# A two-layer decoder trunk on one core: the second block's weights into empty slots, three state sums side by side, and weight sums behind a subtraction

## The chip, the core and the metric

The kernel runs on one core of a Trainium2 chip. The metric is the device time of one execution in microseconds (us), as a median over runs. A core has a matrix engine (TensorE, PE in the rows; its weight loads are PEld), a vector engine (VectorE, DVE), a scalar engine (ScalarE, ACT), GpSimd (POOL) and a queue that issues transfers (SyncE, SP). Each engine works through its own instructions in a fixed order, and an instruction that waits holds up everything behind it on that engine. Matrix products land in PSUM, which has eight banks of 128 x 512 fp32.

## The reference

Two layers run over 592 tokens: 16 learned meta tokens, 8 sample sequences of 8 tokens, and a prompt of 512. The width is 1024 and everything is fp32. Layer 0 has an mLSTM and a retention mixer of four heads each, layer 1 an HGRN2 mixer; behind each mixer stands a ConvFFN of 2816 channels.

```python
xn = rms_norm(x, norm_mix[0])
q_a, k_a, v_a, o_a, i_a, f_a, q_b, k_b, v_b, g = split_cols(xn @ w_in, AB_SIZES)
# mLSTM head, per chunk (retention is alike, with a fixed decay):
num   = (q k^T * d) v + inter * (q @ c0)
c_new = carry * c0 + einsum('bsh,bshd,bshv->bhdv', w, k, v)     # the state sum
h_a   = sigmoid(o_a) * head_layer_norm(num / max(|den|, exp(-m)), g_a)
x     = x + concat([h_a, h_b]) @ w_out
# ConvFFN
u, gate = split(rms_norm(x) @ w_ffn_in)
x = x + (silu(conv3(u)) * gate) @ w_ffn_out
```

The state sum is made once for the 16 meta tokens and once for each of the 8 sample sequences, nine segments in a tile of 80 tokens, and four times for prompt chunks of 128 tokens.

## The kernel before

**Products.** Each fp32 product is three products of rounded halves (hi·hi, hi·lo, lo·hi), gathered in PSUM. Activations stand in SBUF as `h` and `xl`; weights are streamed from memory through SP into `wr` (two buffers). `Split.make` turns a raw piece into `wh`, a cast on ACT (line 302), and `wl`, a subtraction on DVE (line 306). At most three pieces are kept ahead (`pump`).

**Order.** The dense products are one stream of blocks (`stream`), the mixers are others; `interleave` merges them as the program is written, by a clock that `matmul` counts on. The engines' own orders follow from it when the kernel is built, so waits are not written by hand.

**The beginning.** Two blocks of `token_proj` make the values `v` of the four mLSTM heads and their gates. The first takes its weights one k chunk at a time while the tokens come in, sums squares on the way, and then calls `norm_rows`: PE sums the squares (`ssp`), DVE makes the mean (`ms`, line 250) and its reciprocal root (`rt`). Only with `rt` can ACT empty the banks of the first block (`emit_va`: `v_a` line 959, `gtd` line 1042). The second block has its weights in two halves of four k chunks, each a transfer of 512 KB and one of 8 KB (four columns); it calls `norm_bcast` behind its second tile (of five), which spreads `rt` over the partitions (`dg` on DVE, lines 269 and 270, `rbp` on PE, `rb`). Between the transfers of its halves SP loads the table `c_ab` (800 KB, tile `ca`, line 1017), which holds the cosines, sines and masks of the mixers.

**The mixers of layer 0.** `mixer_a(h)` (mLSTM) and `mixer_b(h)` (retention) run for four heads each, about 70 to 300 us into the run. For the sample and meta tokens, `n0_` gathers the numerators, and `seg_update(g, ...)` makes the state sums of nine segments in three bands of partitions:

```python
SEGS = ((0, 32, 3, (0, 1, 2)), (32, 32, 4, (3, 4, 5, 6)), (64, 16, 2, (7, 8)))
```

So `s0` takes rows 0 to 31 and 384 columns, `s1` rows 32 to 63 and 512 columns, `s2` rows 64 to 79 and 256 columns; each is three products (`s<-ve,hi` twice, `s<-ve,lo`). `s0` is written behind `n0_`, then `u`, the sums of the prompt's chunks; `s1` and `s2` come later, ahead of the numerators `na`. All these take one of the four banks of the pool `px`. `upd` adds the sums to the states on DVE (`s_s`, line 1226 or 1304).

**The feed-forward.** Up to 17 of 22 channel blocks of each layer are made by `strassen_block`, which needs sums of weight pieces: `sum12` (`s<-wr`, lines 375 and 376), `sum3` (line 379) and `sum4` (line 383), made on DVE when a `Split` is made. The block's own products go to `ac`, `sb` and `sd`. After `T2`, ACT copies `ac` (line 744), and DVE subtracts (`cs`, line 745); the next block of products into the same bank of `ac` waits for that subtraction.

## Time and profile before

| what | value |
|---|---|
| median of three runs | 1570.47 us (1569.87 to 1573.8) |
| profiled execution, its own time | 1573.42 us |
| span of its trace | 1571.5 us |
| mean granted TensorE clock | 0.995 of full speed (2.4 GHz) |
| busy: PE, DVE, ACT, POOL | 1529.4 (97%), 1147.1 (73%), 731.1 (47%), 193.7 us (12%) |
| bytes moved | 148.57 MB, 95 GB/s on average |

The span runs from the first instruction to the last; 1.9 us of the execution lie around it. Busy is the time in which an engine works on an instruction. All times of the sections below are counted from the start of the span.

### The profile page before, as it was taken

The numbers are of one execution on the slowest core, as the hardware profiler recorded it, in microseconds if no ns is written. First come the engines' busy times: TensorE is split into PE (matmuls) and PEld (weight loads), VectorE is DVE, ScalarE is ACT, GpSimd is POOL, SyncE is SP. The second block draws the span as 40 slices with busy tenths as digits, with TensorE's granted clock in tenths as the row PEclk, the third lists the DMA queues.
The fourth block names the chain that finished last, engine by engine and source line by source line (L and its number), as shares of the span: only waits on it lengthen the run. The fifth ranks groups of instructions, "written<-read, shape, count | busy, mean of one in ns | idle before, by whom it ended". The sixth has DMA issues, their size and how long they took to land. (4 is left out here: it accounts for less than half of the span.)

```text
span 1571.5 us, 32162 instructions
## 1 busy us (share of the span) xinstructions
PE 1529.4 (97%) x13100; PEld 1482.5 (94%) x13100; DVE 1147.1 (73%) x2359; ACT 731.1 (47%) x1325; POOL 193.7 (12%) x399
## 2 busy tenths in 40 slices
PE   7999999999999999999998999999999999999996
PEld 7998999999999999999998798898999999999995
DVE  6676574758987877777547676766689887888875
ACT  6443344334444444445345556564454444444453
POOL 2000000001200000110004524333012000000001
PEclk9999999999999999999999999999999999999998
DMA  7344434433223233224431132223333223233234
GB/s 191 94 100 85 106 95 64 139 95 94 68 81 94 81 95 93 83 76 139 123 94 56 61 93 99 70 84 99 103 100 89 82 81 94 81 97 92 69 109 131
DMA packets 205524, 148.57 MB, mean 95 GB/s; under 512 B 7704, under 2 KB 196888, under 8 KB 205376
## 3 DMA queue, kind: packets, MB, share of 16 engines
q1 hardware_dynamic: 205376, 146.51, 32.7%
q8 instruction: 103, 1.69, 0.4%
q14 instruction: 45, 0.37, 0.1%
HBM read 131.84 MB, written 14.65 MB: 93 GB/s over the span
## 5 line engine op out<-in xcount | busy, mean ns | idle before, releaser
L302 ACT CAST wh<-wr 128x1024 fp32r<-128x1024 f32 (+3 forms) x238 | 230.6, 970 | 357.5 <-PE dp L123 121.1
L306 DVE TENSOR_TENSOR wl<-wr,wh 128x1024 fp32r<-128x1024 f32 (+3 forms) x238 | 268.2, 1127 | 55.4 <-ACT wh L302 50.8
L123 PE MATMUL dp<-h,wh 128*128 128x296 f32 (+1 forms) x1088 | 242.6, 304 | 0.8 <-ACT v_c L959 0.5
L123 PE MATMUL dp<-xl,wh 128*128 128x296 f32 (+1 forms) x1088 | 236.8, 298 | 0.0
L123 PE MATMUL dp<-h,wl 128*128 128x296 f32 (+1 forms) x1088 | 235.6, 298 | 0.0
L123 PE MATMUL dp<-bh,wh 128*128 128x296 f32 (+2 forms) x864 | 188.4, 299 | 0.9 <-DVE x L532 0.5
L123 PE MATMUL dp<-bh,wl 128*128 128x296 f32 (+2 forms) x864 | 186.5, 297 | 0.0
L123 PE MATMUL dp<-bl,wh 128*128 128x296 f32 (+2 forms) x864 | 186.4, 297 | 0.0
L123 PEld LDWEIGHTS dp<-h,wh 128*128 128x128 f32 x1088 | 174.5, 189 | 4.2 <-issue 1.7
L123 PEld LDWEIGHTS dp<-xl,wh 128*128 128x128 f32 x1088 | 176.4, 188 | 0.5 <-issue 0.5
L123 PEld LDWEIGHTS dp<-h,wl 128*128 128x128 f32 x1088 | 176.0, 188 | 0.0
L123 PEld LDWEIGHTS dp<-bh,wh 128*128 128x128 f32 x864 | 139.1, 188 | 3.1 <-issue 1.4
L123 PEld LDWEIGHTS dp<-bh,wl 128*128 128x128 f32 x864 | 139.4, 188 | 0.0
L123 PEld LDWEIGHTS dp<-bl,wh 128*128 128x128 f32 x864 | 139.4, 188 | 0.0
L123 PE MATMUL ac<-h,wh 128*128 128x296 f32 (+1 forms) x408 | 123.3, 302 | 2.6 <-DVE cs L745 2.6
L123 PE MATMUL ac<-xl,wh 128*128 128x296 f32 (+1 forms) x408 | 121.3, 297 | 0.0
L123 PE MATMUL ac<-h,wl 128*128 128x296 f32 (+1 forms) x408 | 121.3, 297 | 0.0
L123 PE MATMUL tp<-wh,h 128*128 128x256 f32 (+3 forms) x280 | 83.3, 302 | 11.9 <-ACT wh L298 6.1
L636 ACT ACTIVATE cv<-cv 128x612 f32<-128x612 f32 (+1 forms) x44 | 31.1, 708 | 116.8 <-DVE cv L632 116.7
L302 ACT CAST wh<-s 128x1024 fp32r<-128x1024 f32 x68 | 56.8, 835 | 59.2 <-PE sb L123 33.0
L123 PEld LDWEIGHTS ac<-h,wh 128*128 128x128 f32 x408 | 76.8, 188 | 4.9 <-DVE cs L745 4.0
L123 PE MATMUL tp<-wl,h 128*128 128x256 f32 (+3 forms) x280 | 80.7, 289 | 0.5 <-DVE wl L299 0.5
(475 smaller groups left out, 3429.0 us busy)
## 6 DMA issues: line engine op xcount, KB each, us to landing
wr<-in_w_ffn_in SPq DMA_DIRECT2D x88, 512.0 KB, 3.8
wr<-in_w_ffn_out SPq DMA_DIRECT2D x32, 512.0 KB, 3.5
wr<-in_w_in_c SPq DMA_DIRECT2D x32, 512.0 KB, 4.0
wr<-in_w_in_ab SPq DMA_DIRECT2D x30, 512.0 KB, 5.9
wr<-in_w_ffn_out SPq DMA_DIRECT2D x24, 384.0 KB, 3.5
x<-in_x SPq DMA_DIRECT2D x16, 296.0 KB, 4.0
out_H<-s_s SPq DMA_DIRECT2D x8, 576.0 KB, 2.8
wr<-in_w_out_ab SPq DMA_DIRECT2D x16, 256.0 KB, 2.7
```

Source lines behind the costliest of these rows:

```text
L123: T.matmul(out, lhsT=lhsT, rhs=rhs, **kw)
L302: S.copy(hi, src)
L306: V.tensor_tensor(out=lo, in0=src, in1=hi.bitcast(F32), op=ALU.subtract)
L636: S.activation(env_["cv"][:, b0:612], env_["cv"][:, b0:612], AF.Silu)
```

## The change

It has three parts.

**1. The beginning.** The second half of the second block's weights no longer waits for a `wr` buffer: it is loaded in two pieces of two k chunks into slots that stand empty then (`bh4`, `bl4`), and each is split by itself. The table `c_ab` is loaded behind these and behind the first weights of the next block. The multiplication of cosines and sines with `rb` moves to the end of `rows()`. Some orders are forced (`behind`): `ms` behind the first half's `wl`, and the next block's weight split behind the second block's work; until then only two pieces are kept ahead.

**2. The state sums of layer 0.** `seg_updates` writes the nine products of the three bands one beside the other into three banks behind `n0_`; `u` gets its bank afterwards. Layer 1 keeps `seg_update`.

**3. The weight sums.** `sum12` is forced behind the subtraction into `cs` (now line 787), and `sum3` and `sum4` become one step.

```diff
+    def behind(i_, other):
+        tc.add_manual_dep(i_.ins, other.ins.name, order_dep, reason="in the order of their use")
...
             if i == 0:
-                V.tensor_scalar(out=ms, in0=p[:, 0:5], scalar1=EPS, scalar2=None, op0=ALU.add)
+                i_ = V.tensor_scalar(out=ms, in0=p[:, 0:5], scalar1=EPS, scalar2=None, op0=ALU.add)
+                if after is not None:
+                    behind(i_, after)
...
+            if isinstance(src, list):
+                hi, lo = (wp.tile([128, self.k, self.n], F32R, name=i, tag=i, bufs=3) for i in ("wh", "wl"))
+                for i, s in enumerate(src):
+                    a, b = i * self.k // len(src), (i + 1) * self.k // len(src)
+                    S.copy(hi[:, a:b, :], s)
+                    V.tensor_tensor(out=lo[:, a:b, :], in0=s, in1=hi[:, a:b, :].bitcast(F32), op=ALU.subtract)
...
+            if places:
+                half = weights([cols(w, c0, b)[:, 0:4, :] for c0, b in pieces])
...
+                    for c0, b in pieces:
+                        next_load(raw[:, :, o:o + b], cols(w, c0, b)[:, 4 + 2 * i:6 + 2 * i, :])
...
-                        norm_rows()
+                        norm_rows(after=live[-1].last if chunks is not None else None)
...
                     hook()
+                    state["ahead"] = 3
+                    pump()
+                    behind(live[-1].first, state["out"])
+                    behind(live[-1].last, state["dg"])
...
         def sum12():
-            V.tensor_tensor(out=s[:, 4:8, :], in0=a21, in1=a22, op=ALU.add)
+            i_ = V.tensor_tensor(out=s[:, 4:8, :], in0=a21, in1=a22, op=ALU.add)
+            if "u2" in state:
+                behind(i_, state["u2"])
...
-                V.tensor_tensor(out=u2, in0=c, in1=u2, op=ALU.subtract)
+                state["u2"] = V.tensor_tensor(out=u2, in0=c, in1=u2, op=ALU.subtract)
...
+    def seg_updates(kt, ve):
+        ps = [px(f"s{g}") for g in range(3)]
+        for i, (k, e) in enumerate(((0, 0), (0, 1), (1, 0))):
+            for p, (r0, m, n, _) in zip(ps, SEGS):
+                matmul(p[:, :n * 128], lhsT=kt[k][r0:r0 + m, :128],
+                       rhs=ve[r0:r0 + m, e, 0:n, :].rearrange("p a b -> p (a b)"), start=i == 0, stop=i == 2)
...
-            ld.dma_start(out=ca[:, 0:1600], in_=I["c_ab"])
+            next_load(ca[:, 0:1600], I["c_ab"])
...
-            n0_, s0, u1 = px("n0_"), px("s0"), px("u1")
+            n0_ = px("n0_")
...
+            sums = seg_updates(kh, ve)
...
+            for p, segs in sums:
+                upd(p, segs)
...
+            u1 = px("u1")
```

How this moves instructions is seen in the engines' orders. On PE at the beginning, before: `tq` takes the products of the second block's first two tiles (80 and 128 tokens), `tp` those of its third; `h_100` to `h_132` are k chunks 0 to 3, of the first half of its weights, and `rbp` is `norm_bcast`.

```order
L123 MATMUL tq<-wh,h_100 128x260
L123 MATMUL tp<-wh,h_100 128x260
L123 MATMUL tq<-wl,h_100 80x260
...
L123 MATMUL tq<-wh,xl_133 128x260
L123 MATMUL rbp<-dg,ones 128x336 x2
L123 MATMUL rbp<-dg,ones 128x256 x2
L123 MATMUL tp<-wl,h_100 128x260
L123 MATMUL tq<-wh,h_143 80x260
```

The same place of the change, where `h_143` to `h_176` are k chunks 4 to 7:

```order
L123 MATMUL tq<-wh,xl_133 80x260
L123 MATMUL tq<-wh,h_143 80x260
...
L123 MATMUL tq<-wh,xl_177 80x260
L123 MATMUL tq<-wl,h_100 128x260
...
L123 MATMUL tq<-wh,xl_177 128x260
L123 MATMUL rbp<-dg,ones 128x336 x2
L123 MATMUL rbp<-dg,ones 128x256 x2
L123 MATMUL tp<-wh,h_100 128x260
```

The third tile's first product stood ahead of the first two tiles' work and now stands behind all of it; all 48 products of these two tiles come ahead of `rbp`, where only the first half of them did. On DVE at the same place, before:

```order
L250 TENSOR_SCALAR ms<-ssp 128x5
L180 TENSOR_SCALAR rs_i<-ms 128x5
...
L189 SCALAR_TENSOR_TENSOR rt<-rs_a,rt 128x5
L269 TENSOR_SCALAR dg<-csm,rt 128x80
L306 TENSOR_TENSOR wl<-wr,wh 128x1040
```

And in the change:

```order
L316 TENSOR_TENSOR wl<-wr,wh 128x1040
L250 TENSOR_SCALAR ms<-ssp 128x5
L301 TENSOR_TENSOR wl<-wr_187,wh 128x520
L180 TENSOR_SCALAR rs_i<-ms 128x5
L181 TENSOR_SCALAR rt<-rs_i 128x5
L301 TENSOR_TENSOR wl<-wr_190,wh 128x520
L187 TENSOR_TENSOR rs_a<-rt 128x5
...
L189 SCALAR_TENSOR_TENSOR rt<-rs_a,rt 128x5
L271 TENSOR_SCALAR dg<-csm,rt 128x80
```

All three subtractions of the second block now stand ahead of the finished `rt`; none did. On PE, the sums of the second mLSTM head, before (`dp` is the dense stream):

```order
L123 MATMUL n__1126<-csm,k_1031 128x9
L123 MATMUL s_1127<-ve,hi 128x384 x2
L123 MATMUL s_1127<-ve,lo 128x384
L123 MATMUL u_1128<-v_a_360,kt 128x129 x3
L123 MATMUL dp<-h_154,wh 128x296 x2
...
L123 MATMUL dp<-h_165,wl 128x296 x2
L123 MATMUL s_1175<-ve,hi 128x512 x2
L123 MATMUL s_1175<-ve,lo 128x512
L123 MATMUL s_1176<-ve,hi 128x256 x2
```

And in the change:

```order
L123 MATMUL n__1137<-csm,k_1052 128x9
L123 MATMUL s_1150<-ve,hi 128x384 x2
L123 MATMUL s_1151<-ve,hi 128x512
L123 MATMUL s_1152<-ve,hi 128x256
...
L123 MATMUL s_1151<-ve,lo 128x512
L123 MATMUL s_1152<-ve,lo 128x256
L123 MATMUL s_1152<-v_a_363,kt 128x129
L123 MATMUL dp<-h_165,wl 128x296
...
L123 MATMUL dp<-h_143,wh 128x296
L123 MATMUL u_1176<-v_a_363,kt 128x129 x3
```

Two visits have become one, and `u`, which followed the first, stands by itself eight products of the dense stream later. The nine products stand together so for four of eight heads (second and third mLSTM head, second and fourth retention head). The first mLSTM head keeps two visits, the widest with two bands; the other three heads have three visits: the three first products, the rest of the third band, the rest of the other two. On DVE in the feed-forward, before:

```order
L306 TENSOR_TENSOR wl<-s_5231,wh 128x512
L375 TENSOR_TENSOR s_5348<-wr 128x512
L376 TENSOR_TENSOR s_5348<-s_5348,wr 128x512
L379 TENSOR_TENSOR wr<-wr 128x512
L306 TENSOR_TENSOR wl<-wr_5237,wh 128x1024
L745 TENSOR_TENSOR cs<-ac,cs 128x296
L383 TENSOR_TENSOR s_5431<-s_5348,wr 128x512
```

And in the change:

```order
L316 TENSOR_TENSOR wl<-s_5179,wh 128x512
L316 TENSOR_TENSOR wl<-wr_5242,wh 128x1024
L787 TENSOR_TENSOR cs<-ac,cs 128x296
L391 TENSOR_TENSOR s_5353<-wr 128x512
L394 TENSOR_TENSOR s_5353<-s_5353,wr 128x512
L794 TENSOR_TENSOR ub<-sb,cs 128x296
L316 TENSOR_TENSOR wl<-wr,wh 128x1024
L397 TENSOR_TENSOR wr<-wr 128x512
```

Three sums that stood ahead of the subtraction into `cs` now stand behind it.

## Rows read from the trace of the kernel before

**Rows 1.** Busy time by stretch: from:to, length, PE, PEld, DVE, ACT, POOL (instructions), clock, DMA.

```profile
0.00:60.00 60.00, 50.19 (x367) 49.13 (x368) 37.82 (x96) 36.15 (x77) 8.56 (x18) 1.00 0.60 160
60.00:310.00 250.00, 249.93 (x1920) 235.01 (x1919) 159.52 (x496) 97.21 (x204) 2.31 (x13) 1.00 0.42 98
```

**Rows 2.** Waits of PE, whole span: what waited, for whom, us, times, longest.

```profile
PE tp L123 <- ACT gtd L1042: 3.2, 2, 1.8
PE ac L123 <- DVE cs L745: 2.6, 3, 1.2
```

**Rows 3.** Timeline of PE at the beginning: start, us, line, operation [idle before <-releaser].

```profile
27.95 0.39 PE L123 MATMUL tp<-wh,h 128*128 128x260 f32 x1 [1.42 <-ACT gtd L1042]
...
39.66 0.39 PE L123 MATMUL tp<-wh,h 128*128 128x260 f32 x1 [1.76 <-ACT gtd L1042]
```

**Rows 4.** Timeline of DVE at the beginning.

```profile
24.29 0.17 DVE L250 TENSOR_SCALAR ms<-ssp 128x5 f32<-128x5 f32 x1 [3.76 <-PE ssp L123]
...
26.50 0.17 DVE L189 SCALAR_TENSOR_TENSOR rt<-rs_a,rt 128x5 f32<-128x5 f32 x1
...
26.88 1.24 DVE L306 TENSOR_TENSOR wl<-wr,wh 128x1040 fp32r<-128x1040 f32 x1
...
29.55 0.61 DVE L270 SCALAR_TENSOR_TENSOR dg<-csm,rt,dg 128x128 fp32r<-128x128 f32 x2
...
32.84 1.18 DVE L1050 TENSOR_TENSOR ca<-ca,rb 128x592 f32<-128x592 f32 x1
```

**Rows 5.** Timeline of ACT at the beginning.

```profile
23.96 1.06 ACT L302 CAST wh<-wr 128x1040 fp32r<-128x1040 f32 x1 [5.47 <-DMA wr<-in_w_in_ab]
26.76 0.47 ACT L959 ACTIVATE v_a<-tp,rt 80x256 f32<-80x256 f32 x1 [1.74 <-DVE rt L189]
```

**Rows 6.** Transfers issued from 14 to 31 us: count, KB each, median us to landing.

```profile
wr<-in_w_in_ab SPq DMA_DIRECT2D x3, 512.0 KB, 6.9
...
wr<-in_w_in_ab SPq DMA_DIRECT2D x2, 8.0 KB, 8.1
```

**Rows 7.** Timeline of PE, sums of the first mLSTM head.

```profile
79.90 0.62 PE L123 MATMUL s<-ve,hi 32*128 32x384 f32 x2
...
80.62 0.94 PE L123 MATMUL u<-v_a,kt 128*128 128x129 f32 x6
...
84.74 0.72 PE L123 MATMUL s<-ve,hi 32*128 32x512 f32 x4
...
85.63 0.49 PE L123 MATMUL s<-v_a,kt 128*128 128x129 f32 x2
```

**Rows 8.** Timeline of PE, sums of the first retention head.

```profile
204.59 0.43 PE L123 MATMUL s<-ve,hi 32*128 32x384 f32 x1
204.95 1.16 PE L123 MATMUL u<-v_b,kt 128*128 128x128 f32 x8
206.04 0.44 PE L123 MATMUL s<-ve,hi 32*128 32x384 f32 x1
...
206.58 0.54 PE L123 MATMUL dp<-xl,wh 128*128 128x296 f32 x2
```

**Rows 9.** Timeline of PE in layer 1, 889.93 to 889.96 us: products on three row bands.

```profile
889.94 0.30 PE L123 MATMUL n__10154<-v_c,near 32*32 32x128 f32 x3
```

**Rows 10.** Timeline of ACT, first retention head.

```profile
203.99 1.28 ACT L883 ACTIVATE ve<-lo,csm 80x128 fp32r<-80x128 f32 x4 [1.24 <-DVE lo L879]
```

**Rows 11.** Timeline of DVE, updates from `s0`, first mLSTM head.

```profile
81.63 0.61 DVE L1226 SCALAR_TENSOR_TENSOR s_s<-s_s,carry,s 128x128 f32<-128x128 f32 x2 [1.17 <-ACT sts L1224]
```

**Rows 12.** Timeline of DVE, first of three waits in the feed-forward.

```profile
620.09 0.69 DVE L375 TENSOR_TENSOR s<-wr 128x512 f32<-128x512 f32 x1 [2.90 <-DMA wr<-in_w_ffn_in]
...
623.16 0.46 DVE L745 TENSOR_TENSOR cs<-ac,cs 128x296 f32<-128x296 f32 x1
```

**Rows 13.** Timeline of ACT, the same place.

```profile
619.07 1.05 ACT L302 CAST wh<-wr 128x1024 fp32r<-128x1024 f32 x1 [2.65 <-PE ac L123]
620.02 0.40 ACT L744 COPY cs<-ac 128x296 f32<-128x296 f32 x1
```

More of the change, by code (lines that the diff above doesn't have):

```diff
@@ L237, in quick_root, with norm_rows @@
         newton(y, x, a)
-    def norm_rows(ts=range(5), root=rsqrt):
+    def norm_rows(ts=range(5), root=rsqrt, after=None):
         p = px("ssp")
@@ L301, in make @@
                 return
-            S.copy(hi, src)
+            self.first = S.copy(hi, src)
             if line:
@@ L305, in make @@
             lo = wp.tile([128, self.k, self.n], F32R, name="wl", tag="wl", bufs=3)
-            V.tensor_tensor(out=lo, in0=src, in1=hi.bitcast(F32), op=ALU.subtract)
+            self.last = V.tensor_tensor(out=lo, in0=src, in1=hi.bitcast(F32), op=ALU.subtract)
             self.made = (hi, lo)
@@ L317, in done @@
             pump()
+    order_dep = mybir.DependencyInfo(mybir.DependencyClass.NoSync, mybir.DependencyReason.DATA)
+    def behind(i_, other):
+        tc.add_manual_dep(i_.ins, other.ins.name, order_dep, reason="in the order of their use")
     line, live = [], []
     def pump():
-        while line and len(live) < 3:
+        while line and len(live) < state.get("ahead", 3):
             line[0].get()
@@ L354, in raw_weights @@
         for a in v:
-            ld.dma_start(out=raw[:, :, o:o + a.shape[2]], in_=a)
+            state["load"] = ld.dma_start(out=raw[:, :, o:o + a.shape[2]], in_=a)
             o += a.shape[2]
@@ L415, in acts_x, with next_load @@
         return [state[c] for c in range(8)]
+    def next_load(out, in_):
+        i_ = ld.dma_start(out=out, in_=in_)
+        behind(i_, state["load"])
+        state["load"] = i_
     def proj(w, c0, post, first=0, hooks=None):
@@ L436, in body @@
                         for a, b in ((0, mid), (mid, NT)):
-                            matmul(p[:, off + a:off + b], lhsT=ww, rhs=xx[:, a:b], start=k == ks[0] and j == 0,
+                            i_ = matmul(p[:, off + a:off + b], lhsT=ww, rhs=xx[:, a:b], start=k == ks[0] and j == 0,
                                    stop=k == ks[-1] and j == 2)
+                            if "tokens" in state:
+                                behind(i_, state.pop("tokens"))
                     if i and k == 7:
@@ L443, in proj_pair, with token_proj @@
         return (lambda: weights(*[[cols(w, c0, 256)[:, k0:k0 + 4, :]] for k0 in (0, 4)]), body)
-    def token_proj(w, pieces, emit, first=False, hook=None, chunks=None):
+    def token_proj(w, pieces, emit, first=False, hook=None, chunks=None, places=None):
         n = sum(b for _, b in pieces)
@@ L462, in load @@
                 return [Split(4, n, r, single=True) for r in raws]
+            if places:
+                half = weights([cols(w, c0, b)[:, 0:4, :] for c0, b in pieces])
+                raws = []
+                for i, tag in enumerate(places):
+                    raw = ap.tile([128, NT], F32, name="wr0", tag=tag)[:, 0:2 * n].rearrange("p (k n) -> p k n", k=2)
+                    raws.append(raw)
+                    o = 0
+                    for c0, b in pieces:
+                        next_load(raw[:, :, o:o + b], cols(w, c0, b)[:, 4 + 2 * i:6 + 2 * i, :])
+                        o += b
+                return half + [Split(4, n, raws)]
             return weights(*[[cols(w, c0, b)[:, k0:k0 + 4, :] for c0, b in pieces] for k0 in (0, 4)])
@@ L468, in products @@
             for i, (a, b) in enumerate(((xh, hi), (xh, lo), (xl, hi))):
-                matmul(out, lhsT=a[:, t0:t0 + r], rhs=b[:, k % 4, :], start=(k == 0 and i == 0),
-                       stop=(k == 7 and i == 2))
+                i_ = matmul(out, lhsT=a[:, t0:t0 + r], rhs=b[:, k % 4, :], start=(k == 0 and i == 0),
+                            stop=(k == 7 and i == 2))
+            return i_
         def body(halves):
@@ L484, in body @@
                     if ts[0] == 0:
-                        norm_rows()
+                        norm_rows(after=live[-1].last if chunks is not None else None)
                 for o in outs:
                     emit(*o)
+                if chunks is not None:
+                    state["ahead"] = 2
                 return
@@ L495, in body @@
                 for k in range(8):
-                    products(p[:r, o:o + n], halves, k, t0, r)
+                    i_ = products(p[:r, o:o + n], halves, k, t0, r)
                     yield
+                if hook is not None and t == 4:
+                    state["tokens"] = i_
                 emit(t, r, p[:, o:o + 512])
@@ L1131, in rows @@
                                 op0=ALU.min)
-            V.tensor_copy(carry.rearrange("p a b -> p (a b)"), p[:, 340:388])
+            done = V.tensor_copy(carry.rearrange("p a b -> p (a b)"), p[:, 340:388])
             gates["rows"] = True
+            for cs in (cosr, sinr):
+                behind(V.tensor_tensor(out=cs, in0=cs, in1=rb, op=ALU.mult), done)
         def post_q(h):
@@ L1227, in upd @@
                                                scalar=carry[:, h, sg - 1:sg], in1=u, op0=ALU.mult, op1=ALU.add)
-            segs = seg_update(0, s0, kh, ve)
+            sums = seg_updates(kh, ve)
             V.tensor_copy(sts[:, 0, 128:129], n0_[:, 256:257])
-            upd(s0, segs)
+            u2 = sums[2][0][:, 256:385]
+            matmul(u2, lhsT=kt[:, 384:512], rhs=v[:, 4, :], start=True, stop=True)
+            for p, segs in sums:
+                upd(p, segs)
+            nn = tiny("nn", 8)
+            V.tensor_tensor(out=nn, in0=c_s[:, 0:8, 128], in1=carry[:, h, 0:8], op=ALU.mult)
+            V.tensor_tensor(out=c_s[:, 0:8, 128], in0=nn, in1=n0_[:, 257:265], op=ALU.add)
+            u1 = px("u1")
             for t in range(3):
@@ L1306, in upd @@
                                        op1=ALU.add)
-            upd(s0, seg_update(0, s0, kh, ve))
+            for p, segs in seg_updates(kh, ve):
+                upd(p, segs)
+            u = px("u")
             for t in range(4):
```

47 lines of the change are left out of this document (18 added, 29 removed).

## The prediction

> **What bounds the kernel now.** Read the busy time by stretch first [rows 1]. From 60 to 310 us, where layer 0's projections and mixers run, PE works 249.93 of 250 us: no wait is there to take away, only PE's own work can become shorter. In the first 60 us it works 50.19, so waits are to be had. Then the list of PE's waits [rows 2]: two of 3.2 us together lie at the beginning, where a product waits for ACT to empty a bank (`gtd`), and three of 2.6 us together wait for DVE's subtraction `cs`; the timeline puts the first of these in the feed-forward of layer 0 [rows 12]. The change works on these three places, and each has its own sum.
>
> **The beginning.** PE waits 1.42 us until 27.95 and 1.76 us until 39.66 [rows 3], 3.18 in all. The first wait is that of the third tile's product, which stands early in PE's order: ACT empties its bank only when `rt` is made (26.67), from 26.76 on [rows 4, 5]. The change puts it behind all 48 products of the first two tiles. PE ran out of work at 27.95 - 1.42 = 26.53, with two of the 48 done; 46 products of 260 columns at the granted 2.4 GHz [rows 1] are 46 x 0.108 = 5.0 us, so it comes to `rbp` at about 31.6 and to the third tile after that.
>
> Is `rbp`'s input `dg` there by then? Now it is finished at 30.16 (29.55 + 0.61), 3.5 us behind `rt`, and 1.24 of that is a `wl` between [rows 4]; without it 2.3. In the change `ms` waits for the first half's `wl`. Its cast waits for a transfer and ends at 25.02 [rows 5]; 1.24 more makes 26.3 instead of 24.29, 2.0 later. Two subtractions of half that size, 0.6 each, also stand ahead of the finished root. So `rt` comes at 26.67 + 2.0 + 1.2 = 29.9 and `dg` at 32.2, if the weights land as now; if they land two us earlier, since the 800 KB table is out of their way, at 27.9 and 30.2. Against 31.6 the stall is 0 to 0.6. I take 0.2. The new weights themselves are wanted by k chunk: chunk 4 some 11 products after 26.53, at 27.7, chunk 6 at 28.4, and by the later of the two cases the two `wl` are ready at about 27.1 and 28.1, which just does.
>
> The second wait is also ACT's: it had other expansions to do ahead of the emission. Third tile, fifth tile, fourth tile is the new order, so a wait there can stay; I leave 0.4 of it. **Term: 3.2 - 0.6 = 2.6 us**, bounds 0 (both waits come back whole) and 3.2. The sine and cosine products leave the beginning, 1.18 for one of them [rows 4] and about 2 for both, and come to DVE at some 72 us; I cost them at nothing, since DVE had 1.17 idle in one gap there [rows 11] and PE did not wait at all in that stretch. With that cover gone they cost up to 2.0. The table itself comes later, but it is read some 40 us after that: nothing.
>
> **The state sums.** In the first mLSTM head `s0` occupies PE from 79.90 to 80.62, 0.72 us, and `s1` with `s2` from 84.74 to 85.63, 0.89 [rows 7]. Three products of 384 columns are 0.48 at 2.4 GHz, three of 512 columns 0.64, and the six of the second visit would be 0.96 one after the other. So two bands already run side by side, and a visit costs its widest band plus about 0.24. The first retention head splits `s0`: 204.59 to 204.95 and 206.04 to 206.58, 0.36 + 0.54 [rows 8]; with 0.89 that makes 1.79 against 1.61. A whole visit of three bands would be 0.64 + 0.24 = 0.88; that three bands can start at once is shown by layer 1, where three products on three bands begin within 0.03 us [rows 9]. A head in three visits costs 0.45 + 0.45 + 0.67 = 1.57 (widest 512, 2 x 256, 2 x 512 columns). By the order: second and third mLSTM heads and the fourth retention head (taken as 1.61) gain 0.73 each, the second retention head 0.91, the first and third retention heads 0.22 each, the fourth mLSTM head 0.04, the first nothing. Sum 3.6.
>
> Two things come off. First, the second and third products need the second half of `ve`: ACT makes all four pieces until 205.27 [rows 10] when PE begins the sums at 204.59. Before, `u` filled that time; where the nine now stand together PE waits about 0.3, and at most 0.7. I take 0.7 for the two retention heads together. Second, three sums and `n0_` fill the pool's four banks, so an mLSTM head's `u` waits for DVE's update from `s0`, which ended at 82.24, 2.3 us after `s0` began [rows 7, 11]. In the order `u` stands behind the sums (0.88), the last chunk's product (0.1) and eight products of the stream (296 columns, 0.12 each): 2.0 to 2.1. That is 0.25 a head, 1.0 for four. **Term: 3.6 - 1.7 = 1.9 us**, bounds 3.6 and, by the fourth rival, a loss.
>
> **The weight sums.** ACT's copy ended at 620.42 [rows 13], but `cs` began at 623.16, behind three sums of which the first had DVE wait 2.90 us for a transfer [rows 12]. `cs` ended at 623.62, and PE's longest wait is 1.2 [rows 2], so PE had run out at 622.4. Now only a `wl` stands ahead of `cs`; its cast ended at 620.12 [rows 13], 1.24 more is 621.4, and `cs` ends at 621.8, 0.6 ahead of PE. Late next are the sums themselves: with their data there at 620.09 they begin at 621.8 instead, 1.7 later. They are wanted by the block's last products and by the next block, two sets of 12 products at the least behind this one; 24 x 0.123 = 3 us. I cost that at nothing; with the cover gone it is up to 1.7 in each of 34 blocks. **Term: 2.6 us**, bounds 0 and 2.9 (a product after a wait is slow to start).
>
> **Sum.** 2.6 + 1.9 + 2.6 = 7.1. From the profiled execution's 1573.4 that leaves 1566.3. Its own time lies 2.95 above the median of the runs shown, so I set the median after at **1563.4 us**.
>
> **The rivals.** (B) *The beginning gives its gain back.* The small transfers of four columns are slow: 8 KB took 8.1 us to land, 512 KB 6.9 [rows 6], and now three of them stand ahead of `rt`. Each us that `dg` comes later than 31.6 is a us of PE. If the last lands three us later than I count, the term is nothing: 1566.0. Against it: they are issued some 4 us earlier than the second half is now.
> The Trainium skill (DMA: Bandwidth & Descriptors, Specifications) has transfers below 512 bytes go by read and modify, and four columns are 16 bytes a row; by that rule these pieces stay the last to land, and the time is that of this rival. The trace agrees so far that the smallest took longest.
>
> (C) *The third band does not run beside the other two.* Then a whole visit costs 0.32 more (three times 256 columns) and a split one about 0.2; with four and three of these the sums gain 3.6 - 1.9 - 1.7 = 0: 1565.3. Rows 9 speak against it, though those products are of 128 columns.
>
> (D) *Slower: `u` waits for the banks.* If it must wait until a head's eight updates are done, not two, at 0.31 each [rows 11], that is 1.9 us more in every head, 15 in eight, against 2.6 + 3.6 + 2.6 = 8.8 gained: 1576.7, or 0.4% slower. It decides at 1.1 us a head, and is slower by more than can be told from 1.7. For it speaks that DVE is dense there; against it, that the retention heads' `u` only follows ACT's copy of `n0_`.
> The Trainium skill (TensorEngine Tiling (Array Packing), PSUM Bottleneck) says that row tiling speeds up TensorE but not the emptying of PSUM, which may then be the bound; that is this rival, and its time by that rule 1576.7. No row of before shows PE waiting for such a bank from 60 to 310 us.
>
> (E) *Nothing that can be measured:* beginning and sums both give back theirs, and only 2.6 remains: 1567.9. (F) *No stall anywhere:* 3.2 + 3.6 + 2.9 = 9.7: 1560.8.
>
> **How the numbers follow.** Chances: mine 0.52, B 0.15, C 0.12, D 0.06, E 0.09, F 0.06. A measurement tells about 0.3% from no change, 4.7 us, so faster means below 1565.8. Of mine 0.50 lies there, of B 0.06, of C 0.08 and F whole: faster 0.70, same 0.24, slower 0.06 (D). The range from 1559 to 1568 leaves out D and the edges of E and F, and goes some 4 us to either side of the likeliest.
>
> **What would show it.** Right: no wait of PE for `gtd` at 28 us and `rbp` at about 32; no waits for `cs` from 600 to 680 us; whole visits of sums of 0.9 us with three bands that start together; 60 to 310 us shorter by about two us with waits under 0.4 for `u`. Wrong would be a wait for `dg` of over one us, visits of 1.2 us and more, waits for `u` of over one us in each head, or new waits in the second feed-forward for the sums that were moved back.

## The result, and the profile after

The changed kernel takes 1563.57 us (median of five runs, 1561.84 to 1565.73) against 1573.34 for the kernel before in the same session: ratio 0.9947, interval 0.9935 to 0.996 (taken over all executions, not from the two medians). Forecast were 1563.4 and "faster". The profiled execution takes 1565.73 us where that of before took 1573.4, so 7.7 less, where 7.1 had been forecast. The total is right; the terms are not, and that they add up is luck (below).

Busy time by stretch, to be held against [rows 1], with two stretches of the feed-forward of layer 0 and of the end:

```profile
0.00:58.00 58.00, 48.86 (x371) 47.36 (x372) 36.60 (x96) 36.84 (x78) 8.66 (x18) 1.00 0.56 165
58.00:308.00 250.00, 249.27 (x1942) 235.39 (x1942) 162.13 (x501) 97.49 (x206) 2.29 (x13) 1.00 0.42 98
600.00:680.00 80.00, 80.00 (x591) 80.00 (x590) 64.93 (x101) 35.06 (x50) 9.99 (x27) 1.00 0.29 86
1500.00:1525.00 25.00, 21.52 (x141) 20.26 (x139) 16.09 (x27) 12.40 (x22) 0.00 (x0) 1.00 0.44 128
1525.00:1530.00 5.00, 4.28 (x20) 4.28 (x21) 1.98 (x3) 1.78 (x3) 0.00 (x0) 0.51 0.34 103
1530.00:1563.90 33.90, 19.95 (x148) 18.81 (x147) 17.92 (x55) 11.07 (x20) 7.32 (x8) 0.80 0.35 113
```

PE's waits in the kernel after; those of [rows 2] on `cs` are gone, that on `gtd` is one, and two belong to the end (`dq`, `rbp` from line 1709):

```profile
PE rbp L123 <- DVE dg L1709: 4.8, 1, 4.8
PE dq L123 <- ACT wh L312: 3.8, 3, 3.1
...
PE tp L123 <- ACT gtd L1096: 1.4, 1, 1.4
...
PE rbp L123 <- ACT gtd L1096: 0.6, 1, 0.6
```

To see where the 7.7 us lie, each product on PE was matched in the two traces with its namesake (same output, inputs and shape, same count of occurrence), and the difference of their starts taken as a median over a stretch of before's time. The difference between two columns is what the stretch between them gained. The kernels of the experiments, described below, stand in the same table (us, kernel less before):

| kernel | 45-65 | 100-130 | 310-330 | 570-600 | 690-710 | 900-1000 | 1200-1230 | 1500-1515 | last product |
|---|---|---|---|---|---|---|---|---|---|
| after | -2.51 | -2.52 | -5.96 | -6.37 | -10.06 | -11.51 | -11.70 | -13.23 | -7.73 |
| e1_beginning | -2.51 | -1.67 | -1.77 | -1.61 | -0.54 | -1.98 | -2.30 | -0.12 | +2.60 |
| e2_sums | +1.32 | +0.20 | -3.24 | -3.24 | -2.49 | -3.96 | -4.37 | -4.42 | -3.81 |
| e3_weights | -0.65 | -0.68 | -0.73 | -0.94 | -4.57 | -5.75 | -6.09 | -7.41 | -4.14 |
| e4_order | -1.66 | -1.69 | -1.72 | -1.98 | -5.61 | -6.88 | -7.20 | -8.52 | -7.43 |
| e7_no_beginning | -2.31 | -3.42 | -6.74 | -6.98 | -10.61 | -11.95 | -10.81 | -12.12 | -11.12 |
| e9_no_beginning_tail | -2.09 | -3.20 | -6.59 | -6.84 | -10.48 | -11.74 | -12.07 | -13.39 | -16.44 |
| e10_before_tail | -0.01 | -0.04 | -0.11 | -0.20 | -0.74 | -2.28 | -2.28 | -2.62 | -5.51 |
| e11_beginning_order | -2.94 | -2.10 | -2.23 | -2.63 | -6.33 | -7.67 | -7.91 | -9.44 | -5.89 |
| e12_beginning_tail | -1.50 | -0.66 | -0.78 | -0.48 | +0.38 | -1.11 | -1.38 | +0.90 | -2.07 |
| e5_tail | -1.92 | -1.93 | -5.37 | -5.73 | -9.43 | -10.98 | -11.25 | -12.78 | -15.96 |
| e8_sel_tail | -4.35 | -4.35 | -7.82 | -8.22 | -11.92 | -13.22 | -13.47 | -15.00 | -18.14 |
| e13_rotary_early | -4.07 | -5.19 | -8.62 | -9.01 | -12.71 | -14.18 | -12.99 | -14.51 | -17.59 |

The row of after reads: 2.5 us in the beginning (hardly any of it by the change, as the next paragraph shows), nothing more to 100 us, 3.4 in the mixers, 0.4 to the feed-forward of layer 0, 3.7 in it, 1.5 in layer 1, 0.2 more, 1.5 in the second feed-forward, and then 5.5 us lost in the last 65. Some 1.2 to 1.5 in layer 1 stand in every row, also in that of e10_before_tail, which changes only the end: they belong to before's profiled execution, in which the granted clock fell there. Its windows from 880:

```profile
880.00:885.00 5.00, 4.12 (x69) 2.75 (x68) 4.19 (x14) 1.54 (x4) 1.43 (x3) 0.69 0.01 3
```

**The beginning.** The 2.5 us stand in the row before anything that the change touches. Products of 260 columns start 0.22 us apart, which is the lower level of 1.2 GHz (260 columns in 0.217), until 14.8 us in before and until 9.4 in after; from there on they start 0.12 apart. PE had begun at 6.13 and at 5.96. The clock column of [rows 1] shows 1.00 for all of this; the starts show both levels. Before, then after:

```profile
14.60 0.42 PE L123 MATMUL tp<-wh,h 128*128 128x260 f32 x1
14.97 0.28 PE L123 MATMUL tp<-wh,xl 128*128 128x260 f32 x1
```

```profile
9.40 0.41 PE L123 MATMUL tp<-wl,h 128*80 128x260 f32 x1 [0.30 <-DVE wl L309]
9.64 0.28 PE L123 MATMUL tp<-wh,xl 128*80 128x260 f32 x1
```

So `ssp`, up to which PE does the same 104 products in both, starts at 23.12 in before and at 20.46 in after, 2.66 earlier: 0.56 of it stand at the product behind the pause (9.96 against 9.40), the rest comes by the clock. From `ssp` to the first product of the dense stream (`dp`) before takes 21.70 us and after 21.85: in this pair of executions the changed stretch gained nothing.

PE comes to `rbp` at 30.65, where 31.6 had been counted, and waits 0.55 ahead of its second half, by the list for ACT's `gtd` and not for `dg`:

```profile
30.65 0.47 PE L123 MATMUL rbp<-dg,ones 128*128 128x336 f32 x2
31.67 0.51 PE L123 MATMUL rbp<-dg,ones 128*128 128x256 f32 x2 [0.55 <-ACT gtd L1096]
...
37.42 0.39 PE L123 MATMUL tp<-wh,h 128*128 128x260 f32 x1 [1.42 <-ACT gtd L1096]
```

The wait at 37.42 is what remains of the second one of [rows 3]. ACT's timeline says why: it stands at the cast of `sel`, whose transfer lies behind the 800 KB table.

```profile
35.65 0.62 ACT L1076 CAST selr<-sel 36x512 fp32r<-36x512 f32 x1 [1.47 <-DMA sel<-in_c_sel]
36.17 0.69 ACT L925 ACTIVATE ve<-v_a,csm 80x128 fp32r<-80x128 f32 x2
36.77 0.46 ACT L1013 ACTIVATE v_a<-tp,rt 128x256 f32<-128x256 f32 x1
37.12 0.25 ACT L1096 ACTIVATE gtd<-tp,rt 128x4 f32<-128x4 f32 x1
```

The transfers issued from 14 to 31 us, beside [rows 6]:

```profile
wr<-in_w_in_ab SPq DMA_DIRECT2D x3, 512.0 KB, 7.8
...
wr<-in_w_in_ab SPq DMA_DIRECT2D x2, 256.0 KB, 8.7
...
wr<-in_w_in_ab SPq DMA_DIRECT2D x2, 4.0 KB, 8.3
```

The 4 KB were nonetheless the last to land: of the last pair the 256 KB were issued at 16.27 and landed at 25.00, the 4 KB at 17.43 and landed at 25.74, and ACT's cast waited for them. Behind it come a `wl`, the finished `rt` and ten emissions of ACT, the last of which ends the wait of 0.55.

```profile
25.82 0.63 ACT L300 CAST wh<-wr 128x520 fp32r<-128x520 f32 x1 [0.84 <-DMA wr<-in_w_in_ab]
```

**The sums.** A whole visit in the second retention head, in PE's timeline: nine products on three bands, and `u` right behind them, 0.88 us later, without a wait.

```profile
215.09 0.73 PE L123 MATMUL s<-ve,hi 32*128 32x384 f32 x6
215.43 0.61 PE L123 MATMUL s<-ve,lo 16*128 16x256 f32 x3
215.97 0.71 PE L123 MATMUL u<-v_b,kt 128*128 128x128 f32 x4
```

**The weight sums.** PE at the first place in the feed-forward, before: from the product ahead of the wait to the one behind it are 1.55 us, while the list counts 1.25, from the end of the product ahead.

```profile
622.13 0.30 PE L123 MATMUL sb<-b2h,wl 128*128 128x296 f32 x1
623.68 0.40 PE L123 MATMUL ac<-h,wh 128*128 128x296 f32 x1 [1.25 <-DVE cs L745]
```

In after the same two start 0.13 apart. DVE's timeline there, after; `cs` now follows `wl`, and the sum behind it waits for nothing:

```profile
613.79 1.23 DVE L316 TENSOR_TENSOR wl<-wr,wh 128x1024 fp32r<-128x1024 f32 x1 [2.95 <-ACT wh L312]
614.93 0.46 DVE L787 TENSOR_TENSOR cs<-ac,cs 128x296 f32<-128x296 f32 x1
615.30 0.68 DVE L391 TENSOR_TENSOR s<-wr 128x512 f32<-128x512 f32 x1
```

**The end.** PE's timeline in the last projection: its last product ends at 1522.63 and the next starts at 1525.72, 3.09 later, when its weights are there; afterwards products of 256 columns follow each other at 0.21 us instead of 0.12, at a granted clock of 0.51 (above), close to the lower level, 1.2 GHz.

```profile
1522.23 0.28 PE L123 MATMUL dq<-bh,wl 128*128 128x256 f32 x1
1522.36 0.28 PE L123 MATMUL dq<-bh,wh 128*128 128x256 f32 x1
1525.72 0.58 PE L123 MATMUL dq<-bh,wh 128*128 128x256 f32 x1 [3.09 <-ACT wh L312]
...
1526.75 0.41 PE L123 MATMUL dq<-bh,wh 128*128 128x256 f32 x1
1526.96 0.41 PE L123 MATMUL dq<-bl,wh 128*128 128x256 f32 x1
```

ACT's cast waited 2.60 us for that piece, so PE's wait is one for a transfer:

```profile
1524.84 0.83 ACT L312 CAST wh<-wr 128x768 fp32r<-128x768 f32 x1 [2.60 <-DMA wr<-in_w_ffn_out]
```

### The profile page after: what moved, and what is told of

It reads as the page before. It is cut to its first block, busy times and chain, and to the rows that moved or that the text cites. A ratio compares the mean times of both kernels' runs of the same rounds, so it can differ in the third digit from the quotient of the medians.

```text
span 1563.9 us, 32095 instructions
## 1 busy us (share of the span) xinstructions
PE 1523.8 (97%) x13100; PEld 1480.0 (95%) x13100; DVE 1144.9 (73%) x2360; ACT 727.1 (46%) x1326; POOL 219.1 (14%) x399
## 3 DMA queue, kind: packets, MB, share of 16 engines
q8 instruction: 103, 1.69, 0.4%
## 5 line engine op out<-in xcount | busy, mean ns | idle before, releaser
L637 POOL COPY cvo<-ub 128x2 f32<-128x2 f32 x44 | 57.2, 1301 | 216.5 <-DVE ub L794 211.9
L123 PE MATMUL sb<-b2l,wh 128*128 128x296 f32 (+1 forms) x272 | 81.1, 298 | 0.0
L123 PE MATMUL sb<-b2h,wh 128*128 128x296 f32 (+1 forms) x272 | 81.0, 298 | 0.0
L123 PE MATMUL sb<-b2h,wl 128*128 128x296 f32 (+1 forms) x272 | 80.9, 297 | 0.0
```

The costliest lines, as they stand in the source:

```text
L123: return T.matmul(out, lhsT=lhsT, rhs=rhs, **kw)
L637: G.tensor_copy(cvo[:, 0:2, fc], ub[:, 612:614])
```

## The experiments

**Each part alone**, and the whole change with a third place for weights at the end. The first three take from the diff only what belongs to their part: e1_beginning the edits of `norm_rows`, `token_proj`, `pump`, `next_load` and the tables; e2_sums

```diff
-            upd(s0, seg_update(0, s0, kh, ve))
+            for p, segs in seg_updates(kh, ve):
+                upd(p, segs)
```

with its like in `mixer_a`; e3_weights

```diff
+            if "u2" in state:
+                behind(i_, state["u2"])
...
-        def sum3():
+        def sum34():
```

and e5_tail gives every third piece of the last projection the free slot `u1` and fetches three pieces ahead:

```diff
-            return (lambda: weights(*views), body)
+                state["fetch"] = 3
...
+                    rs.append(raw_weights(v, turn[0] % 3 == 2))
...
-            while sum(len(w or ()) for w, _ in ahead) < 2:
+            while sum(len(w or ()) for w, _ in ahead) < state.get("fetch", 2):
```

> Part 1 alone, the sums and the weight sums as before. If the parts act each at its own place, the first product of the dense stream behind the token blocks starts at 42.3 us instead of 44.8, all of the rest is shifted by that, and the time is 2.5 us less (ratio 0.9984). If the gain seen at the beginning is only borrowed (an engine that is behind there lets the mixers wait), the stretch up to 310 us ends less than 1 us earlier and the ratio is 0.9995 or more.

> Part 2 alone. If the visits are what counts, layer 0's mixers get 3.4 us shorter, with waits of PE under 0.3 us between 60 and 310 us, and the ratio is 0.9978. If waits for the banks or for the second half of ve eat half of it, as predicted, 1.9 us and 0.9988. If the gain in the mixers came from the earlier beginning, about nothing.

> Part 3 alone. If the three waits for the subtraction were all, 2.6 us from 600 to 680 us and nothing in the second feed-forward (ratio 0.9983). If the order frees DVE also where PE only just did not wait, as the whole change showed, 3.7 us in the first feed-forward and 1.4 to 1.7 in the second: 5.2 us, ratio 0.9967, less what the last 50 us give back.

> The whole change, and in the last block of products (the end of the second feed-forward) every third piece of weights goes to a slot that stands empty there, with three pieces ahead instead of two. If the last 50 us are long because their weights come late and the clock falls to half after that wait, PE's waits for these weights (3.8 us) and the stretch at half clock go, and it is 4 to 6 us faster than the change alone: ratio to before 0.991 to 0.992. If the transfers there are as fast as they can be, the waits stay and the ratio is 0.9947 like that of the change.

| kernel | median, us | ratio to before |
|---|---|---|
| e1_beginning | 1575.96 | 1.0024 (1.0015 to 1.0032) |
| e2_sums | 1566.52 | 0.9972 (0.9963 to 0.9982) |
| e3_weights | 1568.48 | 0.9974 (0.9964 to 0.9984) |
| e5_tail | 1558.58 | 0.9915 (0.9902 to 0.9928) |

The first part alone is slower. Its row in the table shows that it starts its dense stream 2.5 us earlier (2.44 of that stand at `ssp` already, as in after) and then loses in four places: 0.84 by 100 us, 1.07 between 600 and 700, 2.18 between 1230 and 1500, 2.72 at the end. The sums alone gain 4.56 between 65 and 310 us; that their profiled execution starts its dense stream 1.32 later than before's is no effect of theirs: the clock came to the higher level at about 14 us in it and fell to 0.5 again for 3.4 us at 41.0. The third part alone gains 3.6 in the first feed-forward and 1.3 in the second. The third place takes back what the whole change lost at the end: from 1515 on it gains 3.2 where the profiled execution of after, the slowest of its five, lost 5.5; by the ratios it is worth 5.0. PE's wait there is

```profile
PE dq L123 <- ACT wh L312: 0.7, 2, 0.5
```

and with it the stretch at the lower clock behind the wait is gone.

**What of the third part works, and what the beginning is worth in company.** e4_order keeps of the third part only `behind(i_, state["u2"])`, with `sum3` and `sum4` apart as before. e7_no_beginning is the whole change without its first part, e9_no_beginning_tail the same with the third place. e8_sel_tail is e5_tail with another order of loads:

```diff
-            next_load(ca[:, 0:1600], I["c_ab"])
             sel = tmp("sel", 512)[0:36, :]
-            ld.dma_start(out=sel, in_=I["c_sel"])
-            ld.dma_start(out=rm4, in_=I["c_rm"][0:4, :])
-            ld.dma_start(out=gb, in_=I["gate0"])
+            next_load(sel, I["c_sel"])
+            next_load(rm4, I["c_rm"][0:4, :])
+            next_load(gb, I["gate0"])
+            next_load(ca[:, 0:1600], I["c_ab"])
```

> Of the third part only the forced order is kept (the summed weights of the FFN stand behind the subtraction that writes u2); the two later sums stay in two steps, as before. Theory, the order does it: the waits ac <- cs of the first FFN (2.6 us in before) go as they did with the whole third part, and the time is within 0.7 us of the third part alone (ratio 0.997 to 0.998, about 1568.5). Rival, the joined sums do it (the third sum no longer falls between a softmax step and its product): waits ac <- cs of 1 us or more stay and the ratio is 0.9985 to 1.000.

> Parts two and three together, the beginning as before. Theory, the beginning's 2.5 us are kept to the end once the weight sums no longer stall: 2.5 us more than the whole change, 1566 (ratio 0.9962). Rival, what the beginning gains is given back later by weights that meet the stages at another moment, as when it was made alone: the two single ratios multiply, 0.9972 x 0.9974 = 0.9946, about 1563.5, the same as the whole change. If the 4 us that the beginning cost alone were lost in the whole change too, this kernel would be faster than it, below 1561.

> Parts two and three, with the third place for the last projection's weight pieces, and the beginning as before. Theory, the give-back of the last 50 us was the only place in which the beginning's gain was lost: with the third place it is visible, 1558.6 + 2.5 = 1561. Rival, it is lost between 40 and 1500 us: 1558 to 1559, the same as the whole change with the third place.

> The whole change, the third place at the end, and at the beginning the small loads sel, rm and gb ahead of the 800 KB table on SyncE's queue. Theory, the gate work on ScalarE waits for sel behind the table: the wait tp <- gtd (1.4 us in the whole change) goes and 1 us is gained, 1557.5. Rival, the table or the next weights then land later and another wait takes its place: 1558.6 or more.

| kernel | median, us | ratio to before |
|---|---|---|
| e4_order | 1567.78 | 0.9969 (0.9958 to 0.998) |
| e7_no_beginning | 1565.14 | 0.9959 (0.9944 to 0.9974) |
| e9_no_beginning_tail | 1559.28 | 0.992 (0.9906 to 0.9934) |
| e8_sel_tail | 1556.39 | 0.9901 (0.989 to 0.9913) |

The forced order alone does the work of the third part, as the theory had it. With the small loads ahead the wait of PE for `gtd` is gone and e8_sel_tail gains 2.2 us on e5_tail by the medians, more than the 1 us of that wait, though the intervals of the two ratios overlap; the traces below speak for about as much.

What the order takes away is seen on DVE more than on PE. Waits of DVE in the kernel before, first from 560 to 720, then from 1230 to 1500 us:

```profile
DVE s L375 <- DMA wr<-in_w_ffn_in: 15.6, 9, 2.9
```

```profile
DVE s L375 <- DMA wr<-in_w_ffn_in: 21.1, 16, 1.5
```

In e4_order and in after neither row exists any more. In the second stretch PE's busy time says nothing of it: 270.00 of 270 in before as in e4_order, but with 2011 products against 2019. Where the time went is seen when each product's start is held against the start of the one ahead of it. From 570 to 720 us e4_order gains 3.66, and 3.60 of that lie at the first two products that a block writes into `ac` behind products into `sb`, those that wait for `cs`; from 1230 to 1500 us it gains 1.29, all of it at such products, about 0.04 at each of 31 blocks, too little for the list.

e7 and e9 do not tell whether the beginning's gain survives: 0.9959 against 0.9947 and 0.992 against 0.9915, intervals that overlap. Up to 65 us they run the code of before, and yet begin 2.1 to 2.3 us earlier than before's profiled execution: in them too `ssp` comes earlier, at 20.17 and 20.59. In these twelve executions it starts between 20.17 and 23.30, at 21.34 in the mean without the first part as with it. What the first part does is therefore read from `ssp` to `dp`:

| kernels | ssp to dp, us | mean |
|---|---|---|
| without the first part (before, e4, e9, e7, e3, e2, e10) | 21.70, 22.09, 22.14, 22.34, 23.42, 23.54, 23.73 | 22.71 |
| first part (e12, e11, e1, e5, after) | 20.02, 20.70, 21.63, 21.82, 21.85 | 21.20 |
| first part, small loads ahead (e8, e13) | 19.15, 19.82 | 19.49 |

So the first part gains about 1.5 us (0.4 to 2.6, by the spread within the first two groups), and the small loads some 1.7 more. Little of the 1.5 is waits: those for `gtd` sum to 0.8 to 3.5 us in the first group, 2.0 in the mean, and to 1.3 to 2.3 in the second, 1.7 in the mean. In all of the first group but before itself the granted clock fell to 0.5 for 3.4 us, starting between 26 and 41 us; in the second and third group it did not fall there. And from `dp` to the first product of the first head's output (`py`) it takes the same time to 0.02 us whenever the orders are the same:

| kernels | dp to py, us | products |
|---|---|---|
| before, e3, e4, e10 | 52.46, 52.45, 52.45, 52.45 | 402 |
| first part without the sums (e1, e11, e12) | 53.30, 53.30, 53.30 | 402 |
| sums without the first part (e2, e7, e9) | 51.95, 51.95, 51.95 | 409 |
| both (after, e5, e8) | 54.00, 54.00, 54.00 | 414 |

The first part thus gives 0.85 us back alone. Together with the sums five more products of the dense stream stand ahead of `py`, so the 2.05 between the last two rows are not all lost; by the table, whose column 100-130 lies behind that, the first part gives back 1.1 (from the first column on e7 and e9 gain 1.11, after and e5 0.01). All of it comes without a wait of PE. PE's timeline in after shows what has changed: single dense products stand between `b`, `bM` and `bG`, three products of 36 rows.

```profile
73.23 0.38 PE L123 MATMUL b<-mgr,selr 36*128 36x256 f32 x1
73.53 0.40 PE L123 MATMUL dp<-h,wh 128*128 128x296 f32 x1
73.87 0.49 PE L123 MATMUL bM<-mgr,selr 36*128 36x512 f32 x1
74.29 0.40 PE L123 MATMUL dp<-h,wh 128*128 128x296 f32 x1
74.62 0.49 PE L123 MATMUL bG<-mgr,selr 36*128 36x512 f32 x1
75.04 0.54 PE L123 MATMUL dp<-xl,wh 128*128 128x296 f32 x2
```

The sums of the first head are split too: in after they are two visits of 0.72 and 1.13 us with a dense product between, in e7 one of 1.14 (each with two products of `u`'s last chunk).

```profile
79.19 0.61 PE L123 MATMUL s<-ve,hi 32*128 32x384 f32 x2
...
80.25 0.72 PE L123 MATMUL s<-ve,hi 32*128 32x512 f32 x4
```

**Where the beginning alone loses.** e10_before_tail is the kernel before with the third place; e11_beginning_order the first part with the forced order; e12_beginning_tail the first part with the third place.

> The kernel before with only the third place for the last projection's weight pieces, none of the change. Theory, the last projection's waits for weights cost about the same in every order ahead of it: the wait dq <- wh (2.9 us) falls below 1 and rbp <- dg by 0.8, 3 us in all, ratio 0.998. Rival, that give-back belongs to the whole change alone (which reaches the end with its weights later): ratio 0.9995 to 1.0005.

> The first part with the forced order of the weight sums, nothing else. Theory, the beginning alone was slower because it made the FFN's waits for the weight sums longer (3.9 us in 6 waits against 2.6 in 3), and the forced order takes them in either case: 1 to 2 us less than the forced order alone, ratio 0.9955 to 0.9963. Rival, it lost at the end of the kernel and the order doesn't mend that: ratio 0.998 or more.

> The first part with the third place for the last projection's weight pieces, the weight sums as before. Theory, as for the kernel above (the FFN loses): the ratio stays over that of the kernel before with the third place, by 0.0005 or more. Rival, the loss was at the end: with the third place the beginning's 2.5 us show, and the ratio is 0.0015 below that of the kernel before with the third place.

| kernel | median, us | ratio to before |
|---|---|---|
| e10_before_tail | 1567.34 | 0.9972 (0.996 to 0.9985) |
| e11_beginning_order | 1567.79 | 0.9973 (0.9961 to 0.9984) |
| e12_beginning_tail | 1570.7 | 0.9997 (0.9985 to 1.0009) |

With the third place the first part still costs 0.0025 (e12 over e10); with the forced order it costs nothing that can be told (e11 over e4: 0.0004). So it loses mainly in the feed-forwards, by the waits that the order removes: all of what e1 loses against before from 570 to 720 and from 1230 to 1500 us lies at the first two products into `ac`. PE's waits for `cs` in e1_beginning, to be held against [rows 2]:

```profile
PE ac L123 <- DVE cs L787: 3.9, 6, 1.4
```

e11 falls between the two theories: the 1 to 2 us that it should have gained on e4 did not come. By the table its beginning gains 1.28 on e4, gives 0.85 back by 100 us, and at the end it loses 3.55 where e4 loses 1.09. The third place is worth 4.4 us in the kernel before too, more than the 3 us expected, so the end is not a matter of the change alone.

The table also tells the losses at the end apart. The clock fell at the wait for weights in e1, e3, e11 and after, for 3.4 us in the first three and 6.8 in after; they lose 2.7, 3.3, 3.6 and 5.5 us from 1515 on. It did not in e2, e4 and e7, and these lose 0.6, 1.1 and 1.0. How early PE arrives decides neither the wait nor the fall: e1 comes 0.1 us earlier than before and waits 2.8 us, e7 comes 12.1 earlier and waits 2.5.

**The order in the first head.** e13_rotary_early is e8_sel_tail with the two multiplications of the rotary tables back at the beginning:

```diff
+            for cs in (cosr, sinr):
+                behind(V.tensor_tensor(out=cs, in0=cs, in1=rb, op=ALU.mult), ...)
...
-            for cs in (cosr, sinr):
-                behind(V.tensor_tensor(out=cs, in0=cs, in1=rb, op=ALU.mult), done)
```

> The kernel with the small loads ahead and the third place at the end, and of the first part one order taken back: the two multiplications of the rotary tables (cosr and sinr by rb, 0.77 us each on VectorE) stand behind the second block's weight subtraction again and no longer behind the copy into carry at 68.3 us. Theory, the late multiplications keep VectorE from the first head's steps while they run, and the scheduler answers by putting single dense products between b, bM and bG and between s and u, at some 0.1 us for each change of shape: with them early the three stand together again as in the kernel before, and 0.85 to 1.3 us go between 70 and 100 us: 1555.3, ratio 0.9894, the first part's own gain then 1.5 us more at 100 us than with them late. Rival, the loss there has another cause (the smaller distance of PE to the rows' work): the time stays at 1556.4 and the ledger shows the same at 100 us. Rival that ends slower: VectorE waits for the table there and the next subtraction is late, 1557.5 or more with a new wait on wl at 35 to 42 us.

Measured: 1556.98 us, ratio 0.9902 (0.9883 to 0.992), the same as e8_sel_tail by time. The trace decides what the time cannot: in the table it gains 1.12 us from the first column to 100-130, where e8_sel_tail gains nothing; from `dp` to `py` it takes 51.94 us for 409 products instead of 54.00 for 414; the first head's sums are one visit again, from 75.83 to 76.97; and PE's timeline has `b`, `bM` and `bG` together again:

```profile
71.67 0.38 PE L123 MATMUL b<-mgr,selr 36*128 36x256 f32 x1
71.89 0.39 PE L123 MATMUL bM<-mgr,selr 36*128 36x512 f32 x1
72.12 0.39 PE L123 MATMUL bG<-mgr,selr 36*128 36x512 f32 x1
72.44 0.54 PE L123 MATMUL dp<-h,wh 128*128 128x296 f32 x2
72.82 0.44 PE L123 MATMUL dp<-xl,wh 128*128 128x296 f32 x2
```

The three with two dense products take 1.15 us here (71.67 to 72.82) and 1.81 in after (73.23 to 75.04): 0.66 for four more changes between shapes. DVE does the multiplications in a gap in which it would have waited anyway:

```profile
36.04 1.86 DVE L1114 TENSOR_TENSOR ca<-ca,rb 128x592 f32<-128x592 f32 x2
40.64 1.23 DVE L316 TENSOR_TENSOR wl<-wr,wh 128x1024 fp32r<-128x1024 f32 x1 [2.73 <-ACT wh L312]
```

That the profiled execution of e13 is nonetheless not shorter comes from a stretch at a granted clock of 0.82 to 0.84 from 935 to 945 us, which cost it about 1.4. The gain of 1.1 is therefore shown in the trace and not in the median.

## Why the prediction was right in sum and wrong in its terms

**What bounds it.** The three places were the right ones, but not all: the end of the kernel was left out, and there 5.5 us came back in the profiled execution. Its 7.7 us are made of 2.5 that the beginning's change did not make, 1.5 by a fall of the clock in before's execution, 3.7 and 1.5 of the weight sums, 3.4 of the state sums and 0.6 in small pieces, less the 5.5. That 7.1 had been forecast and 7.7 came is luck.

**The beginning, 2.6 forecast.** By the means it was 1.5, and in the profiled pair nothing: the 2.5 there were made ahead of `ssp`, most of them by the clock. The step that failed is the one that took the two waits of a single execution, 3.18, for the difference: in seven executions of the old beginning they sum to 0.8 to 3.5, and with the first part 1.3 to 2.3 stay. The rest of the 1.5 goes with the fall of the clock that six of those seven show. The order itself came as predicted: `rbp` at 30.65 did not wait for `dg`, since `rt` was done at 28.9 and `dg` at 31.7, within the forecast, and the 0.55 of wait were ACT's, which had ten emissions to make behind `rt`. The new weights, which were to "just do", cost waits of 0.52 and 0.39 at 24.38 and 27.23, and the wait left at 37.42 was 1.42, not 0.4. The step "I cost them at nothing" for the sine and cosine products had a cover price of up to 2.0, but looked for it in DVE's gaps and in PE's waits. It came as 0.85 to 1.1 us of PE's own work in another order, at about 73 to 82 us; e13 shows the cause.

**The state sums, 1.9 forecast.** It was 3.4 in the change (-2.51 to -5.96, with what the order in the first head took back already off it), close to the 3.6 that the visits alone were to give, and 4.4 without the first part (e7: from -2.31 to -6.74), where the first head's sums too are one visit, by the prediction's price 0.73 more. The visits were sized rightly: 0.88 for a whole one. The step that failed is that of the two deductions, 0.7 for late `ve` and 1.0 for the banks: no wait of PE for either is in the trace from 58 to 308 us, where it worked 249.27 of 250.

**The weight sums, 2.6 forecast.** It was 3.7 in the first feed-forward and 1.5 in the second. The place and the cause were right; the step "PE's longest wait is 1.2" and the 2.6 taken from the list mis-sized the term. From start to start the three waits cost 3.1 (1.41, 0.47 and 1.21 in e4), because the list counts from the end of the product ahead, and another 0.5 lay at the other first products into `ac`; in the second feed-forward the list had nothing on `cs` at all, while such products lost 1.3 in small steps. DVE had waited 15.6 and 21.1 us for transfers ahead of its subtractions. The new waits feared in the second feed-forward, where the sums come 1.7 us later, did not appear.

**The end, not forecast.** PE waited 3.09 us, against 2.40 at the same place in before, and worked at half the clock after it. The wait is one for weights in two buffers, since a third takes it away (e5, e10), and arriving earlier does not make it longer (e7). Why the clock fell in this kernel and not in e7 stays open.

**The rivals.** B was right on the order of landing and wrong on its price: the 4 KB pieces landed last, 0.74 us behind the 256 KB ones, which were issued 1.16 ahead of them, and the wait of 0.55 at `rbp` hangs on them. By landing 0.74 later they can have cost 0.74 at the most, far from the 2.6 of B. The rule of the Trainium skill (DMA: Bandwidth & Descriptors, Specifications) on transfers below 512 bytes can't be told from this: the 16-byte rows landed last, as it was to be by that rule, but they were also issued last, and took 8.3 us where the others took 8.7. That the beginning gives its gain back is largely true all the same, by the order in the first head. C fell: the three bands start within 7 ns (three rows that begin at 215.09). D fell: no `u` waited. The warning of the Trainium skill (TensorEngine Tiling (Array Packing), PSUM Bottleneck) that the emptying of PSUM may become the bound behind row tiling, named beside D in the prediction, has no wait to show for it in this stretch. E and F lie outside.

**What stays open.** Why the first part makes DVE's waits in the feed-forwards longer (17.4 and 22.3 us in e1 against 15.6 and 21.1) was not tried by itself; all engines work there in the same order as in before, and by e11 the forced order ends it. Why the granted clock fell between 26 and 44 us without the first part and not with it is not shown either. Whether the first part is worth anything within the whole change can't be told from these runs; with the small loads ahead it seems to be (e8 over e9: 0.9901 against 0.992, intervals that just overlap). The best versions are e8_sel_tail and e13_rotary_early, both about 0.99 of the kernel before.

## What to carry to other kernels

When an engine works nearly without pause, compare the number of products and the order of shapes, not only its waits: 0.66 us were lost in one place by putting two dense products between three others, and nothing in the list of waits showed it. A wait costs what lies between the starts of the two products, 1.55 us here where the list had 1.25. Work that one engine does out of the critical path can hold it without a wait being listed there: read the waits of the engine that feeds it (here DVE's 15.6 and 21.1 us for transfers), and look at the last stage too, where a third buffer was worth 4.4 us in the kernel before and 5.0 in the changed one. Before taking a wait of one execution as a term, see by how much that stretch varies between executions: here the first dense product came between 42.5 and 46.1 us without any change of code ahead of it. Compare from a point that both executions reach alike (here `ssp`), not from the start of the span.

## What was not expected of the hardware

The moment at which PE came from the lower to the higher level of its clock differed by more than 5 us between executions of the same code: 9.3 us in e7_no_beginning, 14.9 in before, with the first product at 5.90 and 6.13. This set most of what the starts of `ssp` differ by, 20.17 to 23.30. Later the granted clock fell to about one half in short stretches of every profiled execution. One between 837 and 865 us all have; others moved: 882 us in before, 1525 in after, 1006 in e7_no_beginning, 938 in e13_rotary_early, with 1.4 to 1.5 us lost at 882, 1006 and 938 each. In the last projection it fell at waits of 2.7 (e3), 2.8 (e1), 3.1 (after) and 3.2 us (e11), and not behind 2.4 (before), 2.5 (e7), 2.8 (e2) and 2.9 (e4). So with much the same wait the end lost 0.6 to 1.1 us on before or 2.7 to 5.5, and differences of 1.5 us between single traces are not yet differences between kernels.
